# Row scales of layer 1 applied in three batches, two of them during attention

## The chip, the cores and the metric

One Trainium2 chip, and of it one core. The metric is the device time of one execution of the whole program in microseconds (us). Five engines work on their own instruction streams and wait for each other by semaphores: TensorE (PE in the profile; PEld is its loading of weights), VectorE (DVE), ScalarE (ACT), GpSimd (POOL) and SyncE (SP). Transfers between the chip's memory (DRAM) and the on-chip buffer are issued here by SyncE and ScalarE, each from its own stream and in that stream's order, and run on 16 DMA engines.

## The reference

Two layers on a sequence of 1024 rows of 1024 float32 numbers. Each layer is `x <- x + rmsnorm(mixer(rmsnorm(x)))`. Layer 0's mixer is a retention, layer 1's a differential attention with 16 heads; the change is in layer 1:

```
proj = h @ w_in;  q, k, v, g = split(proj)            # 16 heads, two maps of 64 columns each, v of 128
probs = softmax(q k^T + bias, masked)                 # for each of the two maps
attn  = probs[map 0] - lam * probs[map 1]
out   = rmsnorm(attn @ v, subln_g) * (1 - lambda_init)   # over the 128 columns of a head, row by row
gated = silu(g) * out
y     = gated @ w_out                                 # 2048 x 1024
```

The head's rmsnorm multiplies each row of each head by one number, the row scale.

## The kernel before

Every product is computed in three passes in a rounded 32-bit format: a matrix is split into a high part (a cast on ScalarE) and a low part (a subtraction), and high x high, high x low and low x high are summed. So each weight tile of 128 x 1024 numbers goes through `load_w` (L76): SyncE loads it into a buffer with the tag `raw`, ScalarE casts it (`w_h`, L82) and GpSimd subtracts (`w_l`, L83). The pool `wp` that holds these has two buffers `raw` (L78), three `wh` and three `wl`. A weight's load waits for a free `raw`; its cast waits for a free `wh`, that is for TensorE to be done with the weight three places ahead.

Attention (`attention_layer`, L573) walks through 16 heads with 8 blocks of 128 query rows each, in the order of `ORDER`. TensorE's order is written out by the program itself and kept. Between the steps of a block (logits L729, softmax, transposes L786, value products L800) the program puts pieces of "filler", which is the projection of the coming heads: for head h the query and key weights (here q9, k9 for head 9; L216), the gate weight (g9; L606) and for two heads together two value weights (v5, say; L648). The filler runs at a fixed rate, 40.4 units for each head (L41, L902). The order of the other engines is made by a scheduler; SyncE's and ScalarE's streams are in-order.

A head's output tile leaves unscaled: `values` (L792) makes `go`, `square_sum` (L819) stores it in `self.g1` and adds up its squares, which go to `self.ssd`. The row scales are computed for 12 heads at once when head 12 begins and for the last 4 after attention (`row_scales`, L828): the squares are loaded (L832), the softmax sums transposed (L834), a reciprocal root is taken on VectorE, and the scales are stored in `self.rsd` (L841).

The output stage (`output_stage`, L451) multiplies the gated tiles with the output weights in two halves of 512 columns (hf 0, then hf 1), each over 8 blocks of rows (tb) and 16 tiles (four quarters kq of 4 heads). Whenever a tile is used, it is loaded from `self.g1`, the scales are loaded from `self.rsd`, repeated over 128 partitions, and GpSimd multiplies the two; then come cast and subtraction. `gated8` (L96) does this for 8 heads with the buffers `raw`, `gated` (L460) for 4 with buffers of its own; for the last 4 heads (`LATE`, L40) it also multiplies by the gate, kept apart in `self.sgd` (L471). `WIDE` (L36) says how many quarters of each half go by `gated8`. Some of these products stand already in attention as the last filler (`early` and `heads`, L622, L676).

Of the kernel before, what the change touches and what calls it, by code (L numbers as in the profile page):

```python
# [10 lines left out]
F32 = mybir.dt.float32  # L11
# [8 lines left out]
P = 128  # L20
# [3 lines left out]
TB = T // P  # L24
# [3 lines left out]
DH = 16  # L28
NE = 16
# [21 lines left out]
class _Trunk:  # L51
# [34 lines left out]
    def load_out(self, layer, slots, hf, t, raw=None):  # L86
# [7 lines left out]
        eng.tensor_sub(wl, raw, _f32(wh))  # L94

    def gated8(self, layer, parts):  # L96
        nc = self.nc
        gsrc = self.g0 if layer == 0 else self.g1
        raw = self.wp.tile([P, 8, P], F32, tag="raw", name="w_raw", bufs=2)
        rb = self.wp.tile([P, 8, P], F32, tag="raw", name="w_rb", bufs=2) if layer == 1 else None  # L100
# [12 lines left out]
        return gh, gl  # L113
# [337 lines left out]
    def output_stage(self, layer, slots, nextR, prologue, head):  # L451
        nc, io = self.nc, self.io
        gsrc = self.g0 if layer == 0 else self.g1
        with ExitStack() as es:
# [3 lines left out]
            fp = self.pool(es, "fsb")  # L458

            def gated(tb, kq):  # L460
                raw = fp.tile([P, 4, P], F32, tag="graw", name="graw", bufs=3)
                nc.sync.dma_start(raw, gsrc[tb, :, kq * 4:kq * 4 + 4, :])
                if layer == 1:
                    rb = fp.tile([P, 4, P], F32, tag="rsb", name="rsb", bufs=2)
                    b, k0 = (0, kq * 4) if kq * 4 < BSPLIT else (1, kq * 4 - BSPLIT)
                    nc.sync.dma_start(rb, self.rsd[b][tb:tb + 1, k0:k0 + 4, :].broadcast_to([P, 4, P]))
                    if kq == 3:
                        n = DH - LATE
                        sg = fp.tile([P, n, P], F32, tag="sgl", name="sgl")
                        nc.sync.dma_start(sg, self.sgd[tb])  # L470
                        nc.vector.tensor_mul(raw[:, 4 - n:, :], raw[:, 4 - n:, :], sg)  # L471
                    nc.gpsimd.tensor_mul(raw, raw, rb)  # L472
                gh = fp.tile([P, 4, P], F32R, tag="gh", name="gh", bufs=3)
                gl = fp.tile([P, 4, P], F32R, tag="gl", name="gl", bufs=3 - layer)
                nc.scalar.copy(gh, raw)
                nc.vector.tensor_sub(gl, raw, _f32(gh))  # L476
                return gh, gl

            def product(ps, hf, tb, kq):
                if WIDE[layer][hf] > kq:  # L480
                    if kq % 2 == 0:
                        for _ in self.out_mm(ps, self.gated8(layer, ((tb, kq * 4, 8),)), slots[hf], kq * 4, 8):
                            pass
                    return
                for _ in self.out_mm(ps, gated(tb, kq), slots[hf], kq * 4, 4):
                    pass
# [49 lines left out]
            for tb in range(lead, TB):  # L536
                ps = bank()
# [35 lines left out]
    def attention_layer(self, HR, QR, pmm, ws0, slots):  # L573
        nc, io = self.nc, self.io
        with ExitStack() as es:
# [132 lines left out]
            def batch(h):  # L708
                return (0, h, BSPLIT) if h < BSPLIT else (1, h - BSPLIT, DH - BSPLIT)

# [29 lines left out]
            def softmax_(h, i, Ss):  # L740
# [4 lines left out]
                b, hh, nh = batch(h)  # L745
                col = b * BSPLIT * TB + i * nh + hh
                s0 = s0all[:, col:col + 1]
# [71 lines left out]
            def square_sum(h, j, ob, sqh, sql, go):  # L819
                nc.scalar.dma_start(self.g1[2 * j:2 * j + 2, :, h, :].rearrange("t p q -> p t q"), go.rearrange("p (t q) -> p t q", t=2))  # L820
# [4 lines left out]
                b, hh, nh = batch(h)  # L825
                nc.scalar.dma_start(self.ssd[b][2 * j:2 * j + 2, hh:hh + 1, :].rearrange("t a q -> a t q"), ssr.rearrange("a (t q) -> a t q", t=2))

            def row_scales(b):  # L828
                h0, h1 = (0, BSPLIT) if b == 0 else (BSPLIT, DH)
                n = (h1 - h0) * TB  # L830
# [24 lines left out]
            pend = None  # L855
            rows = None
            ready = 0.0
            ready_o = 0.0
            clk["pe"] = clk["fill"] = 0.0
            for s, (h, i) in enumerate(seq):  # L860
# [41 lines left out]
                n_ = s + 1  # L902
# [6 lines left out]
            if pend is not None:  # L909
                square_sum(*pend)  # L910
            row_scales(1)
            return heads

    def run(self):
# [15 lines left out]
        self.g0 = self.dr.tile([TB, P, NE, P], F32, name="g0")  # L930
        self.g1 = self.dr.tile([TB, P, NE, P], F32, name="g1")
        self.x1d = self.dr.tile([T, D], F32, name="x1d")
        self.sgd = self.dr.tile([TB, P, DH - LATE, P], F32, name="sgd")
        self.ssd = [self.dr.tile([TB, n, P], F32, name="ssd%d" % n) for n in (BSPLIT, DH - BSPLIT)]
        self.rsd = [self.dr.tile([TB, n, P], F32, name="rsd%d" % n) for n in (BSPLIT, DH - BSPLIT)]
        a, b = (lambda i: RA[:, i, :]), (lambda i: RB[:, i, :])
# [112 lines left out]
```

## Time and profile before

| | |
|---|---|
| time, median of 3 runs | 2212.13 us (2209.64 to 2214.02) |
| the profiled execution's own time | 2212.31 us |
| its span, first to last instruction | 2210.5 us |
| TensorE busy | 2145.4 us (97%) |
| mean granted TensorE clock | 0.991 |
| attention ends, output stage begins (last row scales' transpose) | 2012.7 us |

A line of the timeline has start, duration, engine, source line, operation, output and inputs; in brackets stands how long the engine was idle before it and who ended that. A line on waits says who waited for whom, how long in all, how often, and the longest. In the page 40 digits give the busy share of 40 equal slices in tenths. The granted clock is 1.00 at 2.4 GHz and half that at 1.2 GHz.

### The profile page before, as it was taken

The page shows a single profiled execution, that of the slowest core. Times are in us where ns is not written, and L with a number is a line of the kernel's source. Part 1 is how long each engine was busy: PE and PEld are TensorE (multiplying, and loading weights), DVE is VectorE, ACT ScalarE, POOL GpSimd, SP SyncE. Part 2 cuts the span into 40 slices and gives each one's busy share as a digit, 9 for nine tenths or more (in the row PEclk, how much of TensorE's full clock was granted, in tenths as well). Part 3 has the DMA queues.
Part 4 walks back from the last instruction along what each step waited for, and adds up shares of the span by engine and source line. Part 5 has one row for each costly group of instructions (what it writes and reads, how often), then busy time and mean ns, then how long its engine had stood idle before and what let it go on. Part 6 is the DMA issues. An engine that isn't in the chain of part 4 may idle for free. (4 is left out here: it accounts for less than half of the span.)

```text
span 2210.5 us, 31034 instructions
## 1 busy us (share of the span) xinstructions
PE 2145.4 (97%) x11860; PEld 1798.2 (81%) x11860; DVE 1325.3 (60%) x3158; ACT 852.8 (39%) x1648; POOL 471.0 (21%) x260
## 2 busy tenths in 40 slices
PE   7999999999999999999999999999999999998997
PEld 7888988888897888787888888887887888776775
DVE  5264344344436348556776676676676776774765
ACT  4121221221122333345455554555545565542421
POOL 2322411501521000211111111111111111123651
PEclk9999999999999999999999999999999999999999
DMA  4112212112123544311111111111111111145874
GB/s 165 61 39 74 61 35 68 44 50 72 44 72 95 191 153 171 101 41 39 51 39 32 47 50 39 40 50 39 38 40 42 48 41 39 63 136 183 280 251 158
DMA packets 95430, 181.30 MB, mean 82 GB/s; under 512 B 8433, under 2 KB 50609, under 8 KB 95153
## 3 DMA queue, kind: packets, MB, share of 16 engines
q1 hardware_dynamic: 60368, 162.31, 22.6%
q10 hardware_dynamic: 34912, 17.01, 2.5%
q8 instruction: 93, 1.52, 0.3%
q14 instruction: 57, 0.46, 0.1%
HBM read 151.86 MB, written 30.56 MB: 83 GB/s over the span
## 5 line engine op out<-in xcount | busy, mean ns | idle before, releaser
L83 POOL TENSOR_TENSOR w_l<-w_raw,w_h 128x1024 fp32r<-128x1024 f32 x112 | 271.5, 2429 | 1332.1 <-ACT w_h L82 1325.3
L762 ACT ACTIVATE e<-ps_s,nm 128x896 f32<-128x896 f32 (+7 forms) x256 | 189.8, 742 | 105.4 <-DVE nm L760 93.8
L216 PE MATMUL ps_mm<-RB,w_h 128*128 128x512 f32 x512 | 209.5, 409 | 0.3 <-ACT RB L151 0.3
L158 PE MATMUL ps_mm<-RA,w_h 128*128 128x512 f32 x512 | 203.7, 398 | 1.6 <-DVE sg L427 1.6
L159 PE MATMUL ps_mm<-RA,w_h 128*128 128x512 f32 x512 | 204.9, 400 | 0.0
L217 PE MATMUL ps_mm<-RB,w_h 128*128 128x512 f32 x512 | 201.9, 394 | 1.0 <-DVE RB L152 1.0
L218 PE MATMUL ps_mm<-RB,w_l 128*128 128x512 f32 x512 | 202.7, 396 | 0.0
L160 PE MATMUL ps_mm<-RA,w_l 128*128 128x512 f32 x512 | 202.3, 395 | 0.0
L789 ACT CAST ath<-ps_t 128x512 fp32r<-128x512 f32 (+1 forms) x192 | 91.8, 478 | 217.3 <-PE ps_t L786 211.9
L757 DVE TENSOR_REDUCE mx<-ps_s 128x1 f32<-128x640 f32 (+2 forms) x192 | 119.4, 622 | 82.3 <-PE ps_s L732 78.0
L82 ACT CAST w_h<-w_raw 128x1024 fp32r<-128x1024 f32 x112 | 117.6, 1050 | 121.0 <-PE ps_mm L159 33.4
L648 PE MATMUL ps_mm<-w_h,RB 128*128 128x256 f32 x512 | 147.7, 289 | 0.0
L170 PE MATMUL ps_mm<-w_h,RA 128*128 128x256 f32 x512 | 145.8, 286 | 0.0
L168 PE MATMUL ps_mm<-w_h,RA 128*128 128x256 f32 x512 | 145.0, 285 | 0.8 <-ACT RA L151 0.8
L169 PE MATMUL ps_mm<-w_l,RA 128*128 128x256 f32 x512 | 145.1, 284 | 0.1
L650 PE MATMUL ps_mm<-w_h,RB 128*128 128x256 f32 x512 | 143.8, 281 | 0.0
L649 PE MATMUL ps_mm<-w_l,RB 128*128 128x256 f32 x512 | 143.8, 281 | 0.0
L111 ACT CAST g_h<-w_raw 128x1024 fp32r<-128x1024 f32 x50 | 52.5, 1049 | 183.8 <-POOL w_raw L108 81.1
L158 PEld LDWEIGHTS ps_mm<-RA,w_h 128*128 128x128 f32 x512 | 96.2, 188 | 25.2 <-DVE sg L427 2.3
L218 PEld LDWEIGHTS ps_mm<-RB,w_l 128*128 128x128 f32 x512 | 96.2, 188 | 23.6
L112 DVE TENSOR_TENSOR g_l<-w_raw,g_h 128x1024 fp32r<-128x1024 f32 x50 | 71.3, 1427 | 73.0 <-ACT g_h L111 71.0
L160 PEld LDWEIGHTS ps_mm<-RA,w_l 128*128 128x128 f32 x512 | 96.2, 188 | 22.0
(217 smaller groups left out, 5520.9 us busy)
## 6 DMA issues: line engine op xcount, KB each, us to landing
w_raw<-in_wn SPq DMA_DIRECT2D x64, 512.0 KB
w_raw<-g SPq DMA_DIRECT2D x48, 512.0 KB
w_raw<-in_wv SPq DMA_DIRECT2D x32, 512.0 KB
w_raw<-in_wo SPq DMA_DIRECT2D x32, 512.0 KB
xt<-in_x SPq DMA_DIRECT2D x16, 512.0 KB
w_raw<-in_wg SPq DMA_DIRECT2D x16, 512.0 KB
g<-go ACTq DMA_DIRECT2D x32, 256.0 KB
g<-go ACTq DMA_DIRECT2D x64, 128.0 KB
```

The costliest lines, as they stand in the source:

```text
L83: nc.gpsimd.tensor_sub(l, raw, _f32(h))
L158: nc.tensor.matmul(ps, wh[:, k], region[:, kt, cols], start=(kt == 0), stop=False)
L159: nc.tensor.matmul(ps, wh[:, k], region[:, 8 + kt, cols], start=False, stop=False)
L160: nc.tensor.matmul(ps, wl[:, k], region[:, kt, cols], start=False, stop=(kt == KT - 1))
L168: nc.tensor.matmul(ps, region[:, kt, cols], wh[:, k], start=(kt == 0), stop=False)
L169: nc.tensor.matmul(ps, region[:, kt, cols], wl[:, k], start=False, stop=False)
L170: nc.tensor.matmul(ps, region[:, 8 + kt, cols], wh[:, k], start=False, stop=(kt == KT - 1))
L216: nc.tensor.matmul(ps, wh[:, k], HR[:, kt, tok], start=(kt == 0), stop=False)
L217: nc.tensor.matmul(ps, wh[:, k], HR[:, 8 + kt, tok], start=False, stop=False)
L218: nc.tensor.matmul(ps, wl[:, k], HR[:, kt, tok], start=False, stop=(kt == KT - 1))
L648: nc.tensor.matmul(ps[:, t, :], HR[:, kt, cols], wh[:, k], start=(kt == 0), stop=False)
L762: nc.scalar.activation(e[:, 0:n], S[:, 0:n], AF.Exp, bias=nm, accum_out=(s0 if m == 0 else s1))
```

## The change

The heads are scaled in three batches (`BATCHES`: heads 0 to 7, 8 to 11, 12 to 15). The row scales of the first are computed when head 8 begins, of the second when head 12 begins, of the third after attention. During attention a new function `finish` loads the unscaled tiles of a batch and their repeated scales into two `raw` buffers, lets GpSimd multiply them, and stores the final tiles in `self.g1f`; it is called at every second step, 8 times for the first batch (one block of rows each) and 4 times for the second (two blocks each). The output stage loads final tiles and multiplies nothing, except for the last 4 heads in hf 0: these it scales as before and also stores, and hf 1 loads what was stored. In hf 1 all quarters now go by `gated8`.

```diff
-WIDE = ((4, 4), (2, 2))
+WIDE = ((4, 4), (2, 4))
-BSPLIT = 12
+BATCHES = ((0, 8), (8, 12), (12, 16))

+    def gsrc(self, layer, tb, kt, n):
+        if layer == 0:
+            return self.g0[tb, :, kt:kt + n, :]
+        return self.g1f[kt // 8][tb, :, kt % 8:kt % 8 + n, :]
+
+    def finish(self, b, tbs):
+        nc = self.nc
+        h0, h1 = BATCHES[b]
+        n = h1 - h0
+        raw = self.wp.tile([P, 8, P], F32, tag="raw", name="f_raw", bufs=2)
+        rb = self.wp.tile([P, 8, P], F32, tag="raw", name="f_rb", bufs=2)
+        for k, tb in enumerate(tbs):
+            o = slice(k * n, k * n + n)
+            nc.sync.dma_start(raw[:, o, :], self.g1r[b][tb])
+            nc.sync.dma_start(rb[:, o, :], self.rsd[b][tb:tb + 1].broadcast_to([P, n, P]))
+        m = len(tbs) * n
+        nc.gpsimd.tensor_mul(raw[:, 0:m, :], raw[:, 0:m, :], rb[:, 0:m, :])
+        for k, tb in enumerate(tbs):
+            nc.sync.dma_start(self.gsrc(1, tb, h0, n), raw[:, k * n:k * n + n, :])

     def gated8(self, layer, parts):
...
         for tb, kt, n in parts:
-            nc.sync.dma_start(raw[:, o:o + n, :], gsrc[tb, :, kt:kt + n, :])
-            if layer == 1:
-                nc.sync.dma_start(rb[:, o:o + n, :], self.rsd[0][tb:tb + 1, kt:kt + n, :].broadcast_to([P, n, P]))
+            nc.sync.dma_start(raw[:, o:o + n, :], self.gsrc(layer, tb, kt, n))
             o += n
-        if layer == 1:
-            nc.gpsimd.tensor_mul(raw, raw, rb)

-            def gated(tb, kq):
+            def gated(tb, kq, hf):
                 raw = fp.tile([P, 4, P], F32, tag="graw", name="graw", bufs=3)
-                nc.sync.dma_start(raw, gsrc[tb, :, kq * 4:kq * 4 + 4, :])
-                if layer == 1:
+                if layer == 1 and kq == 3 and hf == 0:
+                    nc.sync.dma_start(raw, self.g1r[2][tb])
+                    sg = fp.tile([P, 4, P], F32, tag="sgl", name="sgl")
+                    nc.sync.dma_start(sg, self.sgd[tb])
                     rb = fp.tile([P, 4, P], F32, tag="rsb", name="rsb", bufs=2)
...
+                    nc.sync.dma_start(rb, self.rsd[2][tb:tb + 1].broadcast_to([P, 4, P]))
+                    nc.vector.tensor_mul(raw, raw, sg)
                     nc.gpsimd.tensor_mul(raw, raw, rb)
+                    nc.sync.dma_start(self.gsrc(1, tb, 12, 4), raw)
+                else:
+                    nc.sync.dma_start(raw, self.gsrc(layer, tb, kq * 4, 4))

                 if rows is not None:
                     row_scales(*rows)
+                    todo += [(0, (tb,)) for tb in range(TB)] if rows == (0,) else [(1, (tb, tb + 1)) for tb in range(0, TB, 2)]
                     rows = None
+                elif todo and s % 2 == 1:
+                    self.finish(*todo.pop(0))
...
-                    if i == ORDER[-1] and h == BSPLIT - 1:
+                    if i == ORDER[-1] and h + 1 in (BATCHES[0][1], BATCHES[1][1]):
                         fill_until(ready_o)
                         square_sum(*pend)
                         pend = None
-                        rows = (0,)
+                        rows = (batch(h)[0],)
```

SyncE's stream, before, from the bias tile of head 8 on (`bt`): the three weights are g8, q9 and k9, the next three g9, q10 and k10, the last two v5.

```order
L716 DMA bt<-xd 128x256
L79 DMA w_raw<-in_wn 128x1024 x3
L716 DMA bt<-xd 128x256
L79 DMA w_raw<-in_wn 128x1024 x3
L79 DMA w_raw<-in_wv 128x1024 x2
```

SyncE's stream, now, at the same place: the weights are g8, then q9, then k9; `f_raw`, `f_rb` and `g1f` are the two loads and the store of a `finish`, `g1r` the unscaled tiles, `rsd` the scales.

```order
L729 DMA bt<-xd 128x256
L79 DMA w_raw<-in_wn 128x1024
L729 DMA bt<-xd 128x256
L109 DMA f_raw<-g1r_80 128x1024
L110 DMA f_rb<-rsd_90 128x1024
L114 DMA g1f_83<-f_raw 128x1024
L79 DMA w_raw<-in_wn 128x1024
L109 DMA f_raw<-g1r_80 128x1024
L110 DMA f_rb<-rsd_90 128x1024
L114 DMA g1f_83<-f_raw 128x1024
L79 DMA w_raw<-in_wn 128x1024
```

One `finish` now stands ahead of each of q9, k9, g9, q10, k10 and v5; two more stand between v5 and g10. The second batch has one ahead of each of q13, k13, q14 and k14.

ScalarE's stream, before, at the start of head 12, around the store of the scales (`rsd`): L762 is the softmax exponential, L789 the cast of transposed probabilities, L223 the copy of a projected query.

```order
L789 CAST ath<-ps_t 128x3x128
L659 CAST RA<-ps_mm 128x256
L82 CAST w_h<-w_raw 128x1024
L762 ACTIVATE e,s0all<-ps_s,nm 128x512
L841 DMA rsd_85<-rsr 96x128
L659 CAST RA<-ps_mm 128x256
L762 ACTIVATE e,s_16713<-ps_s,nm 128x512
L789 CAST ath<-ps_t 128x4x128
L223 ACTIVATE RA<-ps_mm 64x512
```

ScalarE's stream, now, at the same place; the two casts of `w_h` are those of q13 and k13.

```order
L775 ACTIVATE e,s0all<-ps_s,nm 128x512
L854 DMA rsd_91<-rsr 32x128
L672 CAST RA<-ps_mm 128x256
L775 ACTIVATE e,s_16799<-ps_s,nm 128x512
L82 CAST w_h<-w_raw 128x1024 x2
L802 CAST ath<-ps_t 128x4x128
L237 ACTIVATE RA<-ps_mm 64x512
L238 ACTIVATE RA<-ps_mm 64x512
L775 ACTIVATE e,s0all<-ps_s,nm 128x1024
```

The cast of k13 now stands ahead of the softmax work and the copies that follow the use of q13. TensorE's own order is the same as before but for the transposes of the sums (at heads 8 and 12 instead of 12 alone) and the place of one sum of squares at head 8.

## Rows read from the trace of the kernel before

**Rows 1.** Page, busy time of each engine, and TensorE's share by slice.
```profile
PE 2145.4 (97%) x11860; PEld 1798.2 (81%) x11860; DVE 1325.3 (60%) x3158; ACT 852.8 (39%) x1648; POOL 471.0 (21%) x260
...
PE   7999999999999999999999999999999999998997
```

**Rows 2.** Busy time by stretch; the first row names the columns.
```profile
core 0: us, PE busy (x) PEld busy (x) DVE busy (x) ACT busy (x) POOL busy (x), PEclk, DMA share, GB/s
1500.00:1587.00 87.00, 85.75 (x460) 69.80 (x458) 61.71 (x162) 47.65 (x100) 11.98 (x5) 1.00 0.14 41
1760.00:1827.00 67.00, 65.42 (x342) 52.47 (x341) 52.51 (x133) 37.72 (x80) 10.11 (x5) 1.00 0.16 50
1920.00:2012.70 92.70, 80.49 (x397) 63.04 (x396) 64.32 (x148) 41.71 (x87) 24.39 (x10) 0.94 0.39 121
2012.70:2202.00 189.30, 171.60 (x698) 134.51 (x696) 123.89 (x184) 49.19 (x81) 85.08 (x45) 0.95 0.73 238
2075.00:2140.00 65.00, 65.00 (x281) 52.29 (x280) 46.44 (x57) 18.81 (x30) 40.44 (x21) 1.00 0.83 269
```

**Rows 3.** TensorE's waits, 2012.7 to 2203: total us, times, longest.
```profile
PE ps_mm L125 <- DVE gl L476: 14.3, 8, 4.1
PE ps_mm L123 <- ACT g_h L111: 2.8, 1, 2.8
```

**Rows 4.** SyncE's queue, 1940 to 2012: start, us to issue, transfer.
```profile
1946.88 0.32 SPq L105 DMA_DIRECT2D w_rb<-rsd  x1
```

**Rows 5.** GpSimd, 1945 to 2015: start, us, operation, idle before it.
```profile
1950.84 2.36 POOL L108 TENSOR_TENSOR w_raw<-w_raw,w_rb 128x1024 f32<-128x1024 f32 x1 [3.98 <-DMA w_rb<-rsd]
```

**Rows 6.** Chain of waits near the end: start, us, what.
```profile
2027.91 1.85 DMA rsd<-rsr
...
2029.78 3.24 DMA rsb<-rsd
...
2170.31 2.63 DMA out<-xt
```

**Rows 7.** Page, ScalarE's casts of weights: busy us, mean ns.
```profile
L82 ACT CAST w_h<-w_raw 128x1024 fp32r<-128x1024 f32 x112 | 117.6, 1050 | 121.0 <-PE ps_mm L159 33.4
```

**Rows 8.** TensorE's timeline at heads 8 and 12, from several stretches.
```profile
1488.01 0.28 PE L822 MATMUL ps_o<-sql,ones 128*128 128x256 f32 x1
...
1500.78 0.40 PE L216 MATMUL ps_mm<-RB,w_h 128*128 128x512 f32 x1
...
1587.06 0.28 PE L648 MATMUL ps_mm<-w_h,RB 128*128 128x256 f32 x1
...
1598.07 0.44 PE L786 MATMUL ps_t<-ident,e 128*128 128x128 f32 x2
...
1752.69 0.31 PE L834 MATMUL ps_t<-ident,s0all 128*96 128x128 f32 x1 [1.40 <-DVE atl L790]
...
1759.55 0.39 PE L216 MATMUL ps_mm<-RB,w_h 128*128 128x512 f32 x1
...
1802.68 0.28 PE L800 MATMUL ps_o<-ath,RA 128*128 128x256 f32 x1
...
1827.30 0.28 PE L648 MATMUL ps_mm<-w_h,RB 128*128 128x256 f32 x1
```

**Rows 9.** ScalarE at head 12, two transfers that it issues.
```profile
1752.13 0.34 ACTq L832 DMA_DIRECT2D rss<-ssd  x1
...
1763.72 0.32 ACTq L841 DMA_DIRECT2D rsd<-rsr  x1
```

**Rows 10.** VectorE at head 12, the scale's reciprocal root.
```profile
1757.81 0.29 DVE L74 SCALAR_TENSOR_TENSOR rsr<-rss,rsr 96x128 f32<-96x128 f32 x1
...
1758.89 1.77 DVE L72 TENSOR_TENSOR rss<-rsr 96x128 f32<-96x128 f32 x1
...
1761.73 1.96 DVE L74 SCALAR_TENSOR_TENSOR rsr<-rss,rsr 96x128 f32<-96x128 f32 x1
```

**Rows 11.** GpSimd at head 12.
```profile
1758.12 2.39 POOL L83 TENSOR_TENSOR w_l<-w_raw,w_h 128x1024 fp32r<-128x1024 f32 x1 [30.36 <-ACT w_h L82]
```

More of the change, by code (lines that the diff above doesn't have):

```diff
@@ L94, in load_out @@
         eng.tensor_sub(wl, raw, _f32(wh))
+    def gsrc(self, layer, tb, kt, n):
[16 more added lines that the diff above has]
+            nc.sync.dma_start(self.gsrc(1, tb, h0, n), raw[:, k * n:k * n + n, :])
     def gated8(self, layer, parts):
         nc = self.nc
-        gsrc = self.g0 if layer == 0 else self.g1
         raw = self.wp.tile([P, 8, P], F32, tag="raw", name="w_raw", bufs=2)
-        rb = self.wp.tile([P, 8, P], F32, tag="raw", name="w_rb", bufs=2) if layer == 1 else None
         o = 0
         for tb, kt, n in parts:
-            nc.sync.dma_start(raw[:, o:o + n, :], gsrc[tb, :, kt:kt + n, :])
-            if layer == 1:
-                nc.sync.dma_start(rb[:, o:o + n, :], self.rsd[0][tb:tb + 1, kt:kt + n, :].broadcast_to([P, n, P]))
+            nc.sync.dma_start(raw[:, o:o + n, :], self.gsrc(layer, tb, kt, n))
             o += n
-        if layer == 1:
-            nc.gpsimd.tensor_mul(raw, raw, rb)
         gh = self.wp.tile([P, 8, P], F32R, tag="wh", name="g_h", bufs=3)
@@ L458, in output_stage @@
             fp = self.pool(es, "fsb")
-            def gated(tb, kq):
+            def gated(tb, kq, hf):
                 raw = fp.tile([P, 4, P], F32, tag="graw", name="graw", bufs=3)
-                nc.sync.dma_start(raw, gsrc[tb, :, kq * 4:kq * 4 + 4, :])
-                if layer == 1:
+                if layer == 1 and kq == 3 and hf == 0:
+                    nc.sync.dma_start(raw, self.g1r[2][tb])
+                    sg = fp.tile([P, 4, P], F32, tag="sgl", name="sgl")
+                    nc.sync.dma_start(sg, self.sgd[tb])
                     rb = fp.tile([P, 4, P], F32, tag="rsb", name="rsb", bufs=2)
[L465 to L471, printed above, removed]
+                    nc.sync.dma_start(rb, self.rsd[2][tb:tb + 1].broadcast_to([P, 4, P]))
+                    nc.vector.tensor_mul(raw, raw, sg)
                     nc.gpsimd.tensor_mul(raw, raw, rb)
+                    nc.sync.dma_start(self.gsrc(1, tb, 12, 4), raw)
+                else:
+                    nc.sync.dma_start(raw, self.gsrc(layer, tb, kq * 4, 4))
                 gh = fp.tile([P, 4, P], F32R, tag="gh", name="gh", bufs=3)
@@ L484, in product @@
                     return
-                for _ in self.out_mm(ps, gated(tb, kq), slots[hf], kq * 4, 4):
+                for _ in self.out_mm(ps, gated(tb, kq, hf), slots[hf], kq * 4, 4):
                     pass
@@ L708, in batch @@
             def batch(h):
-                return (0, h, BSPLIT) if h < BSPLIT else (1, h - BSPLIT, DH - BSPLIT)
+                return next((b, h - h0, h1 - h0) for b, (h0, h1) in enumerate(BATCHES) if h < h1)
             bts = {}
@@ L745, in softmax_ @@
                 b, hh, nh = batch(h)
-                col = b * BSPLIT * TB + i * nh + hh
+                col = BATCHES[b][0] * TB + i * nh + hh
                 s0 = s0all[:, col:col + 1]
@@ L819, in square_sum @@
             def square_sum(h, j, ob, sqh, sql, go):
-                nc.scalar.dma_start(self.g1[2 * j:2 * j + 2, :, h, :].rearrange("t p q -> p t q"), go.rearrange("p (t q) -> p t q", t=2))
+                b, hh, nh = batch(h)
+                nc.scalar.dma_start(self.g1r[b][2 * j:2 * j + 2, :, hh, :].rearrange("t p q -> p t q"), go.rearrange("p (t q) -> p t q", t=2))
                 nc.tensor.matmul(ob[:, 256:512], self.ones, sqh, start=True, stop=False)
@@ L824, in square_sum @@
                 nc.vector.tensor_copy(ssr, ob[0:1, 256:512])
-                b, hh, nh = batch(h)
                 nc.scalar.dma_start(self.ssd[b][2 * j:2 * j + 2, hh:hh + 1, :].rearrange("t a q -> a t q"), ssr.rearrange("a (t q) -> a t q", t=2))
             def row_scales(b):
-                h0, h1 = (0, BSPLIT) if b == 0 else (BSPLIT, DH)
+                h0, h1 = BATCHES[b]
                 n = (h1 - h0) * TB
@@ L856, in attention_layer @@
             rows = None
+            todo = []
             ready = 0.0
@@ L910, in attention_layer @@
                 square_sum(*pend)
-            row_scales(1)
+            assert not todo
+            row_scales(2)
             return heads
@@ L930, in run @@
         self.g0 = self.dr.tile([TB, P, NE, P], F32, name="g0")
-        self.g1 = self.dr.tile([TB, P, NE, P], F32, name="g1")
+        self.g1r = [self.dr.tile([TB, P, h1 - h0, P], F32, name="g1r%d" % h0) for h0, h1 in BATCHES]
+        self.g1f = [self.dr.tile([TB, P, 8, P], F32, name="g1f%d" % k) for k in range(2)]
         self.x1d = self.dr.tile([T, D], F32, name="x1d")
         self.sgd = self.dr.tile([TB, P, DH - LATE, P], F32, name="sgd")
-        self.ssd = [self.dr.tile([TB, n, P], F32, name="ssd%d" % n) for n in (BSPLIT, DH - BSPLIT)]
-        self.rsd = [self.dr.tile([TB, n, P], F32, name="rsd%d" % n) for n in (BSPLIT, DH - BSPLIT)]
+        self.ssd = [self.dr.tile([TB, h1 - h0, P], F32, name="ssd%d" % h0) for h0, h1 in BATCHES]
+        self.rsd = [self.dr.tile([TB, h1 - h0, P], F32, name="rsd%d" % h0) for h0, h1 in BATCHES]
         a, b = (lambda i: RA[:, i, :]), (lambda i: RB[:, i, :])
```

1 line of the change is left out of this document (removed).

## The prediction

> **What bounds the kernel now.** I read the page first: TensorE is busy 97% of the span, and its row of slices is full from the second slice to the last four [rows 1]. So attention, in the middle, has nothing to give, and only what keeps TensorE waiting or spares it a wait counts. Then the stretches [rows 2]. In the middle of attention TensorE is idle 1.25 us of 87 and 1.58 of 67, at full clock; the transfer engines are busy 14 to 16% there and GpSimd 10 to 12 us. In the output stage (2012.7 to 2202) it is busy 171.6 of 189.3 us at a mean granted clock of 0.95, while the transfer engines are busy 73%. A full stretch inside it, 2075 to 2140, loads 280 weights in 65.00 us, 0.232 us each; by that the 696 of the stage need 161.6 us, and 27.7 us are lost: 17.7 of idle time, the rest in work at the half clock of 1.2 GHz behind waits. The waits say what for: 8 for the low part of a gated tile, 14.3 us, and one for a cast, 2.8 us [rows 3]. These tiles come out of load, repeated scale, GpSimd's product, cast and subtraction. In the end of attention (1920 to 2012.7) another 12.2 us are idle, at a clock of 0.94 [rows 2].
>
> **What the change takes away, in the output stage.** 20 loads of repeated scales through `raw` and 20 of the 28 through `rsb`, the 18 GpSimd products of `gated8`, and 20 of the 28 products of `gated` leave the stage and the end of attention; half of the gate products too. hf 1 has then only load, cast and subtraction: one 512 KB load for each 24 matmuls (5.6 us), with three tiles held. I take all its waits as gone. In hf 0 the last four heads keep their chain, with one store more in SyncE's stream, behind which further loads stand; five such tiles follow one another when attention is over, and I leave 5 us for them. So 27.7 - 5 = 22.7 us are gained. In the end of attention the GpSimd products of `gated8` go, the weight copies and the softmax stay: I take 5 of the 12.2 us, bounds 0 and 12. Gain: 27.7 us; bounds 15 and 38.
>
> **What it adds, in attention.** 12 calls of `finish`, each 512 KB of tiles, 512 KB of scales, one GpSimd product and a 512 KB store. No single one of them is much; the order is. In SyncE's stream a `finish` stands ahead of each weight, and it takes both `raw` buffers. So the load of q9 waits in two ways: behind the load of scales, which waits for the row scales, and for the buffer that the store empties.
>
> First the parts. A 512 KB load is issued at 1946.88 and GpSimd starts on it at 1950.84: 3.96 us [rows 4, 5]. The product takes 2.36 us [rows 5]. The small store of the scales takes 1.85 us, a 256 KB store 2.63 us [rows 6]. The store of 512 KB from on-chip memory to DRAM stands nowhere in this trace; it lies between 2.6 and 5.3 us (twice the smaller one), and I take 3.96 like the load, of the same size. The cast is 1.05 us [rows 7].
>
> The Trainium skill ("DMA: Bandwidth & Descriptors", Anatomy of one DMA) gives a transfer 2.0 us plus its bytes at 436 GB/s; for 512 KB that is 3.2 us, an estimate from the page, where the row shows 3.96. By it every round below would be 2.3 us shorter and come under TensorE's pace, which is the second of the rivals; I keep the row.
>
> First batch, head 8. The transposes of the sums now stand 42 gate matmuls, two logits and three sets of transposes ahead of q9. The trace of before has 39 of these matmuls between 1488.1 and 1500.78, 12.7 us [rows 8]; three more matmuls and a few transposes make 13.5 us, and then TensorE wants q9. The scales: at head 12 of before their store is issued 11.0 us behind the transposes (1752.69 to 1763.72) [rows 8, 9]. In it a VectorE instruction of 0.29 us took 1.77 [rows 10] while GpSimd split a weight [rows 11]. Now there is no weight to split at that moment, so I take 1.5 us off: 9.5, bounds 8 and 11. Then 1.85 for the store of scales, 3.96 for their load, 2.36 product, 3.96 store, 3.96 load of q9, 1.05 cast: q9 is there at 26.7 us. **TensorE waits 13.2 us.**
>
> Second batch, head 12. TensorE wants q13 only 6.9 us behind the transposes (1752.69 to 1759.55) [rows 8]. Two transfers instead of one at two places add some 0.7 us of issuing, so q13 is there at 27.3. **TensorE waits 20.4 us.** Before, these weights had been loaded long ahead, and GpSimd's row shows it splitting later ones at that time [rows 11].
>
> Then the rounds. From one weight to the next SyncE needs: low part 2.39 us [rows 11] (until then the next scales have no buffer), scales 3.96, product 2.36, store 3.96, weight 3.96, cast 1.05, with hand-overs 18.0 us. TensorE uses a weight in 17.3 us at heads 8 to 10 (five from 1500.78 to 1587.06) and 16.9 at heads 12 to 14 (four from 1759.55 to 1827.30) [rows 8]. So the lead never comes back while calls of `finish` last. And ScalarE's stream makes it worse: casts of weights that come later stand ahead of exponentials and copies that TensorE needs now, and a cast that waits for its load holds all behind it. Before, the loads were ahead and this cost nothing.
>
> Counted from the cast of q9: k9, g9, q10, k10 and v5 follow at 18.0 each, v5 at 90. Two more calls of `finish` stand between v5 and g10; after v5's second low part (94.8) they take twice 10.3 us, and g10's load and cast 5.0: 120.4. Behind g10's cast stand exponentials whose transposes TensorE had 97.3 us after q9's start (1598.07) [rows 8]; with 2.5 us for them they come at 122.9. **Another 25.6 us are lost.** From q13's cast, with rounds of 18.7: k14 at 56.1, v7's first cast right behind it, 57.2, and then a copy of transposed probabilities that the value products want; these stood 43.1 us after q13's start (1802.68) [rows 8] and come at 58.5. **Another 15.4 us.** Bounds: with a round 1 us shorter or longer these two sums move by 6.5 and 3 us.
>
> GpSimd's 12 products of 2.4 us fall into these waits, and VectorE has room beside them. The half clock behind a wait costs about 1 us here (27.7 - 17.7 us over ten waits); it is swallowed by the next wait but for the last of each batch: 2 us. The 2.8 us that TensorE waited in these stretches before are covered.
>
> **The sum.** 13.2 + 20.4 + 25.6 + 15.4 + 2 - 2.8 = 73.8 us lost, 27.7 gained: 46 us more. The profiled execution took 2212.3 us, 0.2 above the median of the runs; so 2258 us.
>
> **The rivals.**
> - *Faster.* The two buffers are emptied before TensorE notices: the weights ahead of `finish` last until the next is in. For it speak the idle transfer engines and GpSimd in attention [rows 2]. Then the gain of the output stage stands alone: 2212.3 - 27.7 = 2185. Against it: three weights are held, but q13 is wanted 6.9 us behind the transposes, and the scales alone need 11. It decides if the load of q9 or q13 does not wait for the store in front of it. Chance 0.10.
> - *Only the two first waits.* If a round takes less than 17 us, the prefetch recovers after q9 and q13, and the casts hold nothing up. Then 13.2 + 20.4, two waits of 1.9 for the low part and 2 for the clock are lost, 39 us, against the same gain: 2224. By the Trainium skill's figure for a transfer ("DMA: Bandwidth & Descriptors", same section) this would be the case. Chance 0.16.
> - *No gain at all at the end.* The losses as forecast, but in the output stage the stores of the last four heads hold up SyncE's stream, and waits for tiles that have to be stored and loaded again take the place of the old ones: 2212.3 + 74 = 2286. For it speaks that five such tiles are wanted one behind the other, that their loads can only start with the scales, which landed 20.3 us after attention in the trace of before (3.24 us behind 2029.78) [rows 6], and that stores now stand between them. Against it: TensorE has 108 other matmuls first, 25 us at 0.232. Chance 0.11.
>
> The forecast has 0.60. The remaining 0.03 lie within 0.2% (4.4 us, about what a measurement of this kernel tells from no change), between the first two rivals, and count as the same. Faster by more: 0.10. Slower by more: 0.60 + 0.16 + 0.11 = 0.87. The forecast's own range is 2240 to 2276: the rounds move it by 10 us either way, the scales by 3, the gain by 8, not all at once. The range reaches down to most of the second rival and up to nearly the third: 2216 to 2284.
>
> **What would show it.** TensorE's waits would have a wait of 11 to 16 us at q9 and of 18 to 22 us at q13, for the cast of a weight, and several of 2 to 9 us behind them for exponentials and copies; GpSimd would have 12 products of 2.4 us in attention; SyncE's queue would show load of scales, store and weight about 4 us from one another. In the output stage hf 1 would be without waits and the transfer engines well under 73% busy. It is wrong if TensorE goes through heads 8 to 14 without waits of 5 us and more, if the rounds are shorter than 17 us, or if the output stage keeps its waits.

## The result, and the profile after

The changed kernel takes 2230.68 us (median of 4 runs, 2228.13 to 2232.04) against 2210.89 us (4 runs, 2209.51 to 2214.02) for the kernel before: a ratio of 1.0086, 95% interval 1.0069 to 1.0104. It is slower, as forecast, and inside the whole range (2216 to 2284), but outside the forecast's own 2240 to 2276: slower by 19.8 us where 46 were forecast. The places of the loss and of the gain were right; one step of the mechanism, and with it the sizes, was not.

The page: TensorE does the same work, GpSimd has 26 instructions fewer, 38 products in and before the output stage gone and 12 in attention added [rows 1].

```profile
PE 2147.3 (96%) x11861; PEld 1800.0 (81%) x11861; DVE 1288.9 (58%) x3157; ACT 852.3 (38%) x1640; POOL 424.6 (19%) x234
...
PE   7999999999999999999999999998999889998898
```

TensorE's waits over the whole program (line, releaser: total us, times, longest). The first and the last row shown are new: the two weights behind `finish`, and their low parts. The low parts `gl` of the output stage waited 14.3 us before [rows 3], now 6.9.

```profile
PE ps_mm L230 <- ACT w_h L82: 22.4, 2, 14.3
...
PE ps_mm L139 <- DVE gl L489: 6.9, 2, 4.5
...
PE ps_mm L232 <- POOL w_l L83: 2.4, 2, 1.2
```

Where they stand, by TensorE's timeline; these answer to [rows 8]. In turn: transposes of the sums of head 8, first matmul of q9, of v5, transposes of head 12, q13, v7.

```profile
1488.07 0.30 PE L847 MATMUL ps_t<-ident,s0all 128*64 128x128 f32 x1 [1.40 <-DVE atl L803]
...
1510.13 0.80 PE L230 MATMUL ps_mm<-RB,w_h 128*128 128x512 f32 x1 [8.10 <-ACT w_h L82]
...
1605.01 0.28 PE L661 MATMUL ps_mm<-w_h,RB 128*128 128x256 f32 x1
...
1769.70 0.29 PE L847 MATMUL ps_t<-ident,s0all 128*32 128x128 f32 x1 [1.40 <-DVE atl L803]
...
1790.94 0.80 PE L230 MATMUL ps_mm<-RB,w_h 128*128 128x512 f32 x1 [14.31 <-ACT w_h L82]
...
1865.04 0.28 PE L661 MATMUL ps_mm<-w_h,RB 128*128 128x256 f32 x1
```

Against [rows 8] q9 starts 9.4 us later, v5 18.0, q13 31.4 (of which 14.4 are new; 17.0 were left over from the first batch), v7 37.7. The last squares of attention are 33.3 us later (2012.18 before, 2045.45 now), so the end of attention gives 4.4 back. From there to the last matmul it was 189.6 us and is 176.4; the end is 19.7 us later.

The stretches, with the columns of [rows 2]. The first two lie right behind the two long waits and are in part at the half clock; the third is a later stretch of the first batch. The last three are the output stage: all its waits lie in the first two of them, and its last 122 us, which hold all of hf 1, have no wait and run at full clock, the transfer engines at 45% (83% in a full stretch before).

```profile
1510.00:1520.00 10.00, 8.66 (x33) 6.93 (x34) 1.82 (x2) 0.87 (x3) 4.75 (x2) 0.70 0.26 90
1791.00:1800.00 9.00, 7.79 (x19) 5.68 (x20) 0.00 (x0) 0.00 (x0) 4.68 (x2) 0.54 0.18 60
1570.00:1605.00 35.00, 32.77 (x168) 26.19 (x168) 24.40 (x57) 16.88 (x34) 13.02 (x6) 0.95 0.41 145
...
2045.50:2085.00 39.50, 34.67 (x132) 27.29 (x133) 16.01 (x29) 7.69 (x11) 6.46 (x5) 0.89 0.63 202
2085.00:2100.00 15.00, 12.66 (x46) 9.76 (x45) 7.06 (x9) 4.76 (x9) 5.27 (x3) 0.85 0.89 304
2100.00:2222.00 122.00, 122.00 (x524) 98.00 (x523) 60.91 (x129) 32.44 (x51) 10.87 (x5) 1.00 0.45 162
```

So the 37.7 us at v7 are 8.1 and 14.3 at the two weights, 2.4 for their low parts, some 9 of half clock (0.30 of 10 us, 0.46 of 9, 0.05 of 35), and the remaining 4 or so small waits of attention. Of the output stage's 27.7 lost us before, 13.5 are left: 6.9 of waits and 6.6 of half clock (0.11 of 39.5 and 0.15 of 15). About 3.2 of these 6.6 stand in the stage's first 10 us, ahead of its two waits and behind the last waits of attention (granted clock 0.50 from 2045.5 to 2050, 0.81 from 2050 to 2055).

What the prediction got wrong stands in SyncE's queue at q9 (start, us to issue, line, transfer): load of scales, store, weight of q9, the next tile, the next scales, and below them the sixth load of scales.

```profile
1498.31 0.32 SPq L110 DMA_DIRECT2D f_rb<-rsd  x1
1504.45 0.32 SPq L114 DMA_DIRECT2D g1f<-f_raw  x1
1504.86 0.38 SPq L79 DMA_DIRECT2D w_raw<-in_wn  x1
1507.32 0.32 SPq L109 DMA_DIRECT2D f_raw<-g1r  x1
1512.54 0.32 SPq L110 DMA_DIRECT2D f_rb<-rsd  x1
...
1571.10 0.32 SPq L110 DMA_DIRECT2D f_rb<-rsd  x1
```

GpSimd in the same stretch, product and low part of q9:

```profile
1502.07 2.35 POOL L112 TENSOR_TENSOR f_raw<-f_raw,f_rb 128x1024 f32<-128x1024 f32 x1 [49.50 <-DMA f_rb<-rsd]
1510.15 2.35 POOL L83 TENSOR_TENSOR w_l<-w_raw,w_h 128x1024 fp32r<-128x1024 f32 x1 [5.73 <-ACT w_h L82]
```

And ScalarE, the store of the scales and the cast of q9:

```profile
1496.44 0.51 ACTq L854 DMA_DIRECT2D rsd<-rsr  x1
...
1509.03 1.04 ACT L82 CAST w_h<-w_raw 128x1024 fp32r<-128x1024 f32 x1 [2.64 <-DMA w_raw<-in_wn]
```

The scales leave 8.4 us behind the transposes and are loaded from 1498.31; load 3.76 us, product 2.35, then the store, and the weight only 0.41 us behind the store's issue: it does not wait for the store to land. SyncE's waits from 1500 to 1600 say why (line, releaser: total us, times, longest). The load of the next tile (L109) waits for the store; the next scales (L110) wait for the low part of a weight. So the weight takes the buffer of the scales, free with the product, and the next tile takes the one that the store empties. That load is issued 2.9 us behind the store (1504.45 to 1507.32), so the store is also shorter than the 3.96 us put in for it.

```profile
SPq L114 <- POOL f_raw L112: 40.3, 7, 6.0
SPq L110 <- POOL w_l L83: 21.0, 6, 3.9
SPq L109 <- DMA g1f<-f_raw: 11.9, 5, 3.7
```

From the first load of scales to the sixth there is one weight in each round: (1571.10 - 1498.31) / 5 = 14.6 us a round, under TensorE's 17.3. SyncE's waits ahead of the loads of scales (shortest, median and longest in ns, first and last start) show that the first of them held SyncE for 25.2 us, with q9's load behind it.

```profile
L110 SPq EVENT_SEMAPHORE  x7: 17/28/25201, 1473.1 to 1586.2; - x7
```

### The profile page after: what moved, and what is told of

It reads as the page before. It is cut to its first block, busy times and chain, and to the rows that moved or that the text cites. A ratio compares the mean times of both kernels' runs of the same rounds, so it can differ in the third digit from the quotient of the medians.

```text
span 2230.2 us, 30994 instructions
## 1 busy us (share of the span) xinstructions
PE 2147.3 (96%) x11861; PEld 1800.0 (81%) x11861; DVE 1288.9 (58%) x3157; ACT 852.3 (38%) x1640; POOL 424.6 (19%) x234
## 4 chain that ended last, share of the span: by engine, by line
PE 87%; DMA 4%; DVE 4%; ACT 1%; issue 1%; POOL 1%; SPq 0%; ACTq 0%; DVEq 0%; POOLq 0%
PE ps_mm L172 5%; PE ps_mm L173 5%; PE ps_mm L174 5%; PE ps_mm L230 5%; PE ps_mm L232 5%; PE ps_mm L137 5%; PE ps_mm L231 5%; PE ps_mm L139 5%; PE ps_mm L138 5%; PE ps_t L799 3%; PE ps_ret L411 3%; PE ps_mm L661 3%; PE ps_mm L663 3%; PE ps_mm L662 3%; PE ps_s L742 3%; PE ps_mm L182 3%
## 5 line engine op out<-in xcount | busy, mean ns | idle before, releaser
L230 PE MATMUL ps_mm<-RB,w_h 128*128 128x512 f32 x512 | 212.2, 415 | 22.7 <-ACT w_h L82 22.4
L231 PE MATMUL ps_mm<-RB,w_h 128*128 128x512 f32 x512 | 204.1, 399 | 1.0 <-DVE RB L166 1.0
L126 DVE TENSOR_TENSOR g_l<-w_raw,g_h 128x1024 fp32r<-128x1024 f32 x58 | 78.5, 1354 | 97.5 <-ACT g_h L125 94.6
L230 PEld LDWEIGHTS ps_mm<-RB,w_h 128*128 128x128 f32 x512 | 98.2, 192 | 41.6 <-ACT w_h L82 23.1
L125 ACT CAST g_h<-w_raw 128x1024 fp32r<-128x1024 f32 x58 | 60.7, 1048 | 170.1 <-PE ps_mm L138 124.3
L172 PEld LDWEIGHTS ps_mm<-RA,w_h 128*128 128x128 f32 x512 | 96.2, 188 | 25.2 <-DVE sg L441 2.3
```

The lines of the kernel that those rows point to most:

```text
L172: nc.tensor.matmul(ps, wh[:, k], region[:, kt, cols], start=(kt == 0), stop=False)
L230: nc.tensor.matmul(ps, wh[:, k], HR[:, kt, tok], start=(kt == 0), stop=False)
L231: nc.tensor.matmul(ps, wh[:, k], HR[:, 8 + kt, tok], start=False, stop=False)
```

## The experiments

All runs in one table, each with its ratio to the kernel before on the same chip. "Attention" is from the transposes of head 8 (1488.01 before [rows 8]) to the last squares, "output" from there to the last matmul, both from TensorE's timeline of one profile; profiles of one and the same stage differ by up to 5 us, so small effects are read from the times.

| kernel | us | ratio to before, 95% | attention | output |
|---|---|---|---|---|
| before, in all rounds | 2210.89 to 2212.54 | 1 | 524.2 | 189.6 |
| changed | 2230.68 | 1.0086 (1.0069 to 1.0104) | 557.4 | 176.4 |
| later | 2206.69 | 0.9977 (0.9966 to 0.9988) | 532.5 | 174.4 |
| no_finish | 2193.10 | 0.9918 (0.9903 to 0.9932) | 518.4 | 173.9 |
| no_scales_wait | 2201.40 | 0.9960 (0.9947 to 0.9973) | 533.6 | 171.8 |
| two_products | 2239.36 | 1.0125 (1.0108 to 1.0142) | 564.6 | 174.4 |
| three_products | 2257.75 | 1.0205 (1.0189 to 1.0221) | 585.7 | 172.0 |
| spaced | 2198.55 | 0.9934 (0.9920 to 0.9947) | 524.6 | 173.9 |
| graw4 | 2229.87 | 1.0075 (1.0060 to 1.0091) | 557.4 | 173.4 |
| spaced_graw4 | 2202.96 | 0.9956 (0.9944 to 0.9969) | 529.7 | 177.9 |
| interleaved | 2204.01 | 0.9957 (0.9944 to 0.9971) | 524.6 | 179.8 |
| one_more_ahead | 2198.16 | 0.9936 (0.9922 to 0.9949) | 525.0 | 173.3 |
| gate_on_gpsimd | 2193.87 | 0.9915 (0.9899 to 0.9931) | 525.7 | 170.0 |
| gate_on_gpsimd_ahead | 2197.09 | 0.9929 (0.9911 to 0.9946) | 523.3 | 173.0 |

**Where the loss sits: no_finish, later, no_scales_wait.** The edit of no_finish:

```diff
-nc.scalar.dma_start(self.g1r[b][2 * j:2 * j + 2, :, hh, :]...
+dst = self.g1r[b][...hh, :] if b == 2 else self.g1f[h // 8][2 * j:2 * j + 2, :, h % 8, :]
...
-                    todo += [...]
...
-                elif todo and s % 2 == 1:
-                    self.finish(*todo.pop(0))
```

of later:

```diff
-                    rows = None
-                elif todo and s % 2 == 1:
+                    rows, due = None, s + 3
+                elif todo and s >= due and s % 2 == 1:
```

and of no_scales_wait:

```diff
-nc.sync.dma_start(rb[:, o, :], self.rsd[b][tb:tb + 1].broadcast_to([P, n, P]))
+nc.sync.dma_start(rb[:, o, :], self.g1r[b][tb])
```

> No `finish` at all: heads 0 to 11 store their gated tiles straight to the final tensors, unscaled (this kernel leaves out the product with the row scales for these heads). It prices the output stage's gain by itself. Both theories: attention runs as before (q9, q13 within 1 us) and ends some 4 us earlier, near 2008 us; the output stage is as in the changed kernel, 175 us up to the last matmul against 189, so the time is near 2193 us (2188 to 2198). If the first-wait theory holds, the kernel with the later `finish` comes within 8 us of this one; if the rounds cost the time, it is 25 us or more above it.

> The first `finish` of each batch is called two steps later, so that the weight of q9 (and of q13) stands ahead of it in SyncE's stream; all else is as in the changed kernel. Theory (the changed kernel loses its time at the two first weights, which stand behind a load that waits for the row scales, and rounds of about 14.75 us cost nothing against a pace of 17): the waits of 8.1 and 14.3 us are gone, q9, v5, q13 and v7 start within 4 us of the kernel before, attention ends near 2010 us and the kernel near 2196 us (2191 to 2204). Rival (the rounds themselves cost it: 12 products, 36 more transfers of 512 KB beside attention): the lag still grows to 25 us or more by v7, and the time stays at 2222 to 2232 us.

> `finish` stays where it is, with all its loads, products and stores, but its second load takes the gated tile once more in place of the row scales (the product is then a square: the scaling of heads 0 to 11 is left out), so that nothing in SyncE's stream waits for the scales. Theory of the first waits: SyncE no longer stands 25 us for one load, q9 and q13 are there in time, waits of at most 2 us, the time is 2193 to 2206 us. Rival (contention or the rounds): the same transfers and products run, so the time stays at 2222 to 2232 us.

Without `finish` the time is 2193.10 us, as expected: this is what the rest of the change gains, 19 us, and the changed kernel pays 37.6 us for the calls. Both other kernels have neither of the two waits, with all transfers and products in place (the second load of no_scales_wait brings the same number of bytes from another tensor): 24.0 us back by the order alone, 29.3 without the wait for the scales. So the rival that the rounds themselves cost the time is out for the greater part. But 'later' missed its expectation (2191 to 2204) by 2.7 us, and both stay above 2193 by 8 to 14 us. Its waits in attention, 1480 to 1900:

```profile
PE ps_t L799 <- DVE e L781: 6.6, 7, 1.7
PE ps_t L799 <- DVE atl L803: 5.9, 2, 3.3
```

and the same without `finish`, where the sum for `e` is half and the waits for `atl` are nearly gone:

```profile
PE ps_t L799 <- DVE e L781: 3.5, 4, 1.7
...
PE ps_t L799 <- DVE atl L803: 0.4, 1, 0.4
```

ScalarE of 'later' ahead of one of them (TensorE waits 2.66 us up to 1560.72): the cast of a weight stands 3.17 us for its load, and attention's squares and copies stand behind it.

```profile
1555.63 1.05 ACT L82 CAST w_h<-w_raw 128x1024 fp32r<-128x1024 f32 x1 [3.17 <-DMA w_raw<-in_wn]
1556.59 0.38 ACT L821 ACTIVATE sq<-ps_o 128x256 f32<-128x256 f32 x1
...
1557.92 0.59 ACT L802 CAST ath<-ps_t 128x512 fp32r<-128x512 f32 x1 [0.52 <-DVE mx L770]
```

**What a round costs: two_products, three_products.** The product of `finish` is done two or three times.

```diff
-        nc.gpsimd.tensor_mul(raw[:, 0:m, :], raw[:, 0:m, :], rb[:, 0:m, :])
+        for _ in range(2): nc.gpsimd.tensor_mul(raw[:, 0:m, :], raw[:, 0:m, :], rb[:, 0:m, :])
```

> `finish` multiplies twice (the tiles of heads 0 to 11 come out scaled by the square), so each round has 2.35 us more on GpSimd between load and weight. Theory (rounds cost only what they exceed TensorE's pace of 17.3 and 16.9 us by): a round goes from 14.75 to 17.1 us, the two first waits grow by 2.35 us each to about 10.5 and 16.7 us, and the rounds add 0 to 8 us in all: 2240 us (2234 to 2246). Rival (every round's time passes on to TensorE, so 12 x 2.35 us): 2259 us (2252 to 2266).

> Three products in each `finish` of the changed kernel (heads 0 to 11 come out with the scales' third power). Theory (a round costs what it exceeds TensorE's pace by): a round is 14.75 + 4.7 = 19.45 us, over the pace of 17.3 and 16.9; the two first waits grow by 4.7 us each to 12.8 and 19 us, and the some five and three rounds of the batches that have a weight behind them cost 2.2 and 2.5 us each: 2258 us (2250 to 2268). Rival (each 2.35 us costs as much as the first one did, 8.7 us for all rounds together, with no threshold): 2248 us.

Both came out as expected: 2239.36 us (2240 expected), and 2257.75 (2258). The waits at q9 and q13 are 10.45 and 16.93 us in the first, 13.03 and 19.59 in the second. The first and the sixth load of scales, with two products, (1587.14 - 1500.79) / 5 = 17.3 us a round:

```profile
1500.79 0.32 SPq L110 DMA_DIRECT2D f_rb<-rsd  x1
...
1587.14 0.32 SPq L110 DMA_DIRECT2D f_rb<-rsd  x1
```

and with three, 20.3:

```profile
1499.27 0.32 SPq L110 DMA_DIRECT2D f_rb<-rsd  x1
...
1600.86 0.32 SPq L110 DMA_DIRECT2D f_rb<-rsd  x1
```

The first 2.35 us a round, up to TensorE's pace of 17.3, cost 8.7 us: 5.0 of them are the growth of the two first waits, the rest was not traced apart (the waits for `e` in attention grow from 6.6 to 9.5 us). The second, above the pace, cost 18.4, of which 5.2 are growth of the first waits: TensorE now waits at later weights as well, in the waits of three_products from 1480 to 1900 (four waits for the weights of q and k instead of two, and low parts of weights):

```profile
PE ps_mm L230 <- ACT w_h L82: 36.0, 4, 19.6
...
PE ps_mm L232 <- POOL w_l L83: 6.8, 5, 1.7
PE ps_mm L621 <- POOL w_l L83: 3.4, 2, 1.7
```

**The rest of attention: spaced.** As 'later', and

```diff
-                elif todo and s >= due and s % 2 == 1:
+                elif todo and s >= due and s % 4 == 3:
```

> The first `finish` two steps later, as in the run 'later', and one in every fourth step instead of every second, so that a weight without a `finish` ahead of it lies between two rounds. Theory (the 14 us that 'later' still loses in attention against the kernel without `finish` come from casts of late weights, which wait in ScalarE's stream for their load and hold attention's own work behind them, as the 3.17 and 2.57 us there): with more lead the casts wait no more, attention comes within 5 us of the kernel without `finish`, and the time is 2195 to 2201 us. Rival (the products on GpSimd slow VectorE, wherever they lie; their number is the same): 2204 to 2209 us.

2198.55 us, inside the theory's range: 8.1 us less than 'later', with the same products on GpSimd. The waits for `atl` in attention fall from 5.9 to 1.5 us:

```profile
PE ps_t L799 <- DVE atl L803: 1.5, 1, 1.5
```

Attention is 6.2 us longer than without `finish`, against 5 expected. ScalarE's waits for loads of weights, 1480 to 1900, in 'later' (the first two rows) and in 'spaced' are halved, not gone; without `finish` there are none.

```profile
ACT w_h L82 <- DMA w_raw<-in_wn: 12.7, 8, 3.2
ACT w_h L82 <- DMA w_raw<-in_wv: 4.6, 3, 2.6
...
ACT w_h L82 <- DMA w_raw<-in_wn: 8.9, 7, 2.5
```

But the spacing changes something else too. For the same work in attention VectorE is busy 371.9 us without `finish`, 377.9 in 'later' and 373.4 in 'spaced'. In 'later' VectorE's `sql` took 1.82 us (its median is 0.42) beside a low part on GpSimd, up to 1559.42 and so into the wait of 2.66 us shown above, and the `atl` that TensorE waited for stood behind it:

```profile
1557.60 1.82 DVE L823 TENSOR_TENSOR sql<-sq,sqh 128x256 fp32r<-128x256 f32 x1
...
1556.76 2.37 POOL L83 TENSOR_TENSOR w_l<-w_raw,w_h 128x1024 fp32r<-128x1024 f32 x1 [7.32 <-ACT w_h L82]
```

So the 8.1 us are shown to come from the spacing; how much of them is ScalarE's stream and how much VectorE beside GpSimd, no run tells apart.

**The output stage: graw4, spaced_graw4, interleaved, one_more_ahead.** The edit of graw4, which also takes one buffer `gh` away:

```diff
-raw = fp.tile([P, 4, P], F32, tag="graw", name="graw", bufs=3)
+raw = fp.tile([P, 4, P], F32, tag="graw", name="graw", bufs=3 + layer)
...
-gh = fp.tile([P, 4, P], F32R, tag="gh", name="gh", bufs=3)
+gh = fp.tile([P, 4, P], F32R, tag="gh", name="gh", bufs=3 - layer)
```

spaced_graw4 is the same on top of 'spaced'; so is this, interleaved:

```diff
-                for tb in range(lead):
+                ahead = {1: 5, 3: 6, 4: 7}
+                for tb in range(TB):
                     product(head[tb], 0, tb, 3)
                     first(tb, head[tb])
+                    if tb in ahead:
+                        head.append(bank())
+                        for kq in range(3):
+                            product(head[ahead[tb]], 0, ahead[tb], kq)
+                lead = TB
```

and this, one_more_ahead:

```diff
-                head.append(bank())
-                for kq in range(3):
-                    product(head[lead], 0, lead, kq)
-                lead += 1
+                for _ in range(2):
+                    head.append(bank())
+                    for kq in range(3):
+                        product(head[lead], 0, lead, kq)
+                    lead += 1
```

> The changed kernel, but in layer 1's output stage the narrow tiles have four buffers `graw` instead of three (and two `gh` instead of three, for the room). Theory (TensorE's waits of 4.54 and 2.34 us there come from the third buffer: the load of the fourth of the five last quarters waits for a store to land, VectorE waits for that load, and the low part of the third stands behind it): the first wait goes, the second stays at 2.3 us or less, and with the half clock behind them 3 to 9 us go: 2226 us (2222 to 2228). Rival (the row scales come too late whatever the buffers): waits as before, 2229 to 2232 us.

> Both edits in one kernel. If their gains add, 2192 us (2187 to 2198), some 20 us under the kernel before; if the waits in the output stage come from the scales, as 'spaced'.

> 'spaced', and in layer 1's output stage the last quarters (heads 12 to 15) of hf 0 no longer follow one another five times: behind those of row blocks 1, 3 and 4 stand the first three quarters of blocks 5, 6 and 7, 36 matmuls or 8.4 us each; the same work in another order. Theory (a last quarter takes about 7 us of loads, two products, store and copies and is wanted every 2.8 us, and this, not the row scales alone, keeps the output stage from its full gain): the two waits of 5.00 and 1.21 us and the half clock behind them go, 6 to 11 us: 2190 us (2186 to 2194). Rival (each wait only moves to the next of these tiles, since SyncE issues all loads in one order): 2196 to 2201 us.

> 'spaced', and one more row block's first three quarters (8.4 us of matmuls) stand ahead of the first last quarter; six last quarters then follow one another instead of five. By the same theory 8.4 us more of cover stand against one more tile of about 7 us for 2.8 us of matmuls, so the waits shrink by some 4 us of the 6.2 and do not go: 2194 us (2190 to 2198). If the waits came from the landing of the row scales alone, 8.4 us of cover take all of them and the half clock: 2189 us.

The theory fell in the first three, and the fourth gives it no support. graw4: 2229.87 us, the rival's time, the waits 5.75 and 0.61 us instead of 4.54 and 2.34. spaced_graw4: 2202.96, rather slower than 'spaced' alone. interleaved: 2204.01, with three waits of 5.61, 2.14 and 3.33 us; they moved on, which the rival had said, and were 4.9 us longer in all than the two of 'spaced', which it had not. one_more_ahead: 2198.16, just outside its range of 2190 to 2198 and the time of 'spaced', though its waits are 1.82 and 2.60 us instead of 5.00 and 1.21. VectorE's timeline of graw4 shows that one buffer more does not take the wait away (what it is worth with three `gh` was not tried): the gate product of a later tile (L481) still waits 6.62 us for its load, which SyncE issues only at 2072.08 behind other transfers, and two finished tiles wait behind it for their low parts (L489).

```profile
2079.03 1.20 DVE L481 TENSOR_TENSOR graw<-graw,sgl 128x512 f32<-128x512 f32 x1 [6.62 <-DMA graw<-g1r]
2080.15 1.21 DVE L126 TENSOR_TENSOR g_l<-w_raw,g_h 128x1024 fp32r<-128x1024 f32 x1
2081.28 2.36 DVE L489 TENSOR_TENSOR gl<-graw,gh 128x512 fp32r<-128x512 f32 x2
```

**VectorE's stream: gate_on_gpsimd, gate_on_gpsimd_ahead.** The first is 'spaced' with this edit, the second has 'one_more_ahead' as well.

```diff
-                    nc.vector.tensor_mul(raw, raw, sg)
+                    nc.gpsimd.tensor_mul(raw, raw, sg)
```

> 'spaced', with the gate product of the last four heads in the output stage on GpSimd instead of VectorE. Theory (TensorE's waits there are for low parts that are ready to be worked out, but stand in VectorE's stream behind the gate product of a later tile, which waits for its load: 6.62 us in the run with four buffers, 3.67 in the changed kernel): VectorE has no gate product left to wait at, the second tile's low part comes some 4 us earlier, the first wait falls from 5.00 to 0.5 to 2 us and the half clock behind it goes: 2192 us (2188 to 2196). Rival (the tiles themselves are late, so the wait stays wherever the product runs): 2196 to 2201 us.

> 'gate_on_gpsimd' and 'one_more_ahead' together: with VectorE free of the gate products and 8.4 us more cover, by the theory all waits of the first last quarters go: 2190 us (2186 to 2194). By the rival the row of six tiles is still 7 us each against 2.8 and nothing changes: 2196 to 2201 us.

2193.87 us (2192 expected), the fastest kernel here that leaves nothing out: 0.85% under the kernel before (interval 0.69 to 1.01%). Against 'spaced' the medians differ by 4.7 us, but the intervals of the two ratios overlap. And the mechanism was only half right. The second wait is gone and the first is 4.11 us, not 0.5 to 2:

```profile
PE ps_mm L139 <- DVE gl L489: 4.1, 1, 4.1
```

VectorE now waits in the same place for something else: the low part of a wide tile (L126) whose copy `g_h` is late. By the order of the program it is that of row block 7, which TensorE wants only after blocks 5 and 6; the two narrow low parts that it wants now stand behind.

```profile
2044.40 1.25 DVE L126 TENSOR_TENSOR g_l<-w_raw,g_h 128x1024 fp32r<-128x1024 f32 x1 [6.11 <-ACT g_h L125]
2045.58 1.28 DVE L489 TENSOR_TENSOR gl<-graw,gh 128x512 fp32r<-128x512 f32 x2
```

With one more block ahead it was 2197.09 us, against 2190 expected: that block gave nothing in either kernel. TensorE waits there 4.29 and 1.54 us for casts, and for the first of these tiles GpSimd had itself waited 8.86 us for the load, which speaks for the rival:

```profile
PE ps_mm L137 <- ACT gh L488: 5.8, 2, 4.3
...
2061.29 1.26 POOL L481 TENSOR_TENSOR graw<-graw,sgl 128x512 f32<-128x512 f32 x1 [8.86 <-DMA graw<-g1r]
```

Whether the wait left in gate_on_gpsimd can be had by another order on VectorE was not tried.

## Why the prediction was right in sign and wrong in size

- **The two first weights: right in place, too large: 33.6 us forecast, 22.4 measured.** TensorE wanted q9 14.0 us behind the transposes (13.5 forecast) and q13 6.9 (6.9). They were there at 22.1 and 21.2 us, where 26.7 and 27.3 were forecast. The step that failed is *"the load of q9 waits ... for the buffer that the store empties"*, and with it the 3.96 us of the store in the chain: q9 takes the buffer of the scales, and its load was issued 0.41 us behind the store. The rest is the scales' own store, 8.4 and 7.7 us behind the transposes instead of 9.5. So 8.1 and 14.3 us of waiting instead of 13.2 and 20.4. No row of before had a 512 KB store, as the prediction said; the one here gave its buffer back 2.9 us behind its issue, but to the next tile and not to q9.
- **The rounds: wrong, by the same step.** The store's 3.96 stood in each round too. 18.0 forecast, 14.6 measured, and that is on the other side of TensorE's 17.3 and, by the prediction's own sign (rounds shorter than 17 us), means that it is wrong. So the lead came back, and of 25.6 and 15.4 us forecast behind the two first weights the lag grew by 7.6 (17.0 left of it at q13, less 9.4 at q9) and 6.3. That the sum turns on this was right: in three_products, with rounds driven over the pace and first waits of 13.0 and 19.6 us, the lag grows at later weights too. That its 2257.75 us are the 2258 forecast is luck: its rounds are 20.3 us and not 18.0, its attention is 61.5 us longer than before where 68.8 were forecast, and its output stage gains 17.6 and not 22.7.
- **ScalarE's stream: seen, its price not shown.** A cast that waits for its load does hold attention's squares and copies up ('later'). Spacing the rounds gave 8.1 us back, but a part of that may be VectorE beside GpSimd, which the prediction took as free.
- **The half clock: 2 us forecast, about 9 measured.** It was to be swallowed by the next wait; as the rounds were short there was none, and each long wait cost 3 to 4 us more.
- **The end of attention: right** (5 forecast, 4.4; all of attention is 5.8 us shorter without `finish`).
- **The output stage: gain mis-sized.** hf 1 has no wait at all, as forecast, but for the five last quarters 5 us were left and 13.5 are lost there. That finished tiles are held up in VectorE's stream was not foreseen (taking the gate products out of it gave 4.7 us between the medians, with overlapping intervals), nor the half clock: some 3 us at the stage's start and as much around its two waits. So the gain is 13.2 us (189.6 to 176.4), not 22.7.
- **The rivals.** *Only the two first waits* was closest in its mechanism: rounds under 17 us. That its 39 us lost are near the 37.7 measured is luck: its first waits were 11.2 us too large, and the half clock and small waits of attention made up for it. Its 2224 us failed on the smaller gain. It did not come about by the Trainium skill's figure ("DMA: Bandwidth & Descriptors", Anatomy of one DMA), which is given there for transfers that GpSimd issues. Here SyncE issues them, and the 512 KB loads took 3.76 us (scales, issue to product) and 4.17 (weight, issue to cast), near the 3.96 of before and not the 3.2 of the page. *Faster* had its condition met, the load of q9 did not wait for the store, and was still wrong: the wait for the scales in SyncE's stream was enough. *No gain at all at the end* did not happen.

## What to carry to other kernels

Before a chain is added up, follow which instruction frees each buffer and who takes it next: here one store wrongly put in the chain was 4 of 18 us a round and put the rounds on the wrong side of the pace of what they feed, from which a repeated cost counts (2.35 us a round cost 8.7 us up to it, 18.4 above). A load that waits for another engine's result holds everything behind it on its queue; put it behind the loads that are wanted soon (24 us here for a shift by two steps), and leave rounds of prefetch free between such loads (8 us more). When waits on an in-order engine are removed, look at what it waits for next before counting the gain.

## What was not expected of the hardware

TensorE ran at the half clock of 1.2 GHz for some us behind each long wait: granted clock 0.70 in the 10 us behind the wait of 8.1, 0.54 in the 9 us behind that of 14.3; the cost, 3.0 and 4.1 us, came on top of the waits. VectorE's `sql` took 1.82 us beside a low part on GpSimd where its median is 0.42. And the same attention code, in 'spaced' and in spaced_graw4, took 524.6 and 529.7 us in two profiles; why is open.
